# A hybrid decoder layer: gate products on half the array's rows, and two chunks' weight sums on another engine

## The chip, the cores and the metric

The kernel runs on one core of a Trainium2 chip. The core has five engines that work beside each other: TensorE (PE; its weight loads are listed apart as PEld), VectorE (DVE), ScalarE (ACT), GpSimd (POOL) and SyncE (SP), which here only issues DMAs. ScalarE and GpSimd issue a few DMAs too. The metric is the device time of one execution in microseconds (us); a profile of one further execution shows what each engine did and when.

## The reference

One layer over 1040 tokens (16 learned meta tokens and 1024 inputs) of width 1024, in float32:

```python
u = rmsnorm(h, g_pre_mix)
z = u @ w_in                                  # q | k | v | x_rec | y_rec
attn = sliding_window_attention_with_sinks(q, k, v, sinks)   # 8 heads, window 128
xr = causal_depthwise_conv(x_rec, conv_w, conv_b)            # 512 channels
gate_r = einsum("btnc,ncd->btnd", xb, w_a) + b_a             # 8 blocks of 64 channels
gate_i = einsum("btnc,ncd->btnd", xb, w_x) + b_x
r, i = sigmoid(gate_r), sigmoid(gate_i)
log_a = -8 * r * softplus(-lam);  a = exp(log_a)
hr = scan(a, sqrt(1 - a * a) * (i * xr))                     # h_t = a_t h_(t-1) + u_t
mix = concat([attn, gelu(y_rec) * hr]) @ w_out
h = h + rmsnorm(mix, g_post_mix)
f = square(relu(rmsnorm(h, g_pre_ffn) @ w_ff1)) @ w_ff2      # 1024 -> 4096 -> 1024
out = (h + rmsnorm(f, g_post_ffn))[16:]
```

Each of the two gates multiplies 8 separate blocks of 64 channels by a matrix of 64x64 of its own.

## The kernel before, in words

**Products in three parts.** Every float32 operand is split into a high part (a ScalarE copy to fp32r, line 96) and a low part (VectorE, source minus high part, line 99), and `mm3` (lines 123 to 129) multiplies high by high, high by low, low by high into one PSUM bank. So each product in the profile stands three times, at L125, L126 and L127, and each operand costs one ScalarE and one VectorE pass.

**Order.** A scheduler orders each engine's instructions by data dependence and a priority. The helper `behind` (line 106) adds an order without a wait across engines; `lut` (line 81) chains the ScalarE table functions in program order. Buffers are slots of a tag with a fixed number (line 55: two for "raw", four for "ws" and "d", two for "e", eight for "c", and so on); a load into a slot waits until the last reader of the old content is done, and SP's queue is worked in order.

**First stage, up to about 200 us.** Norm, transposes and the input projection; then attention over four head pairs. `scores` makes the scores, the softmax and the divisions on ScalarE and VectorE; `attend` transposes the probabilities on TensorE, splits them (L96, L99), masks both parts with GpSimd selects (L609) and multiplies by V (L620). Between them TensorE works on "fills" (`next_fill`, line 694): projections of the q, x and y columns (`project`), whose results are copied out of PSUM (y: L676 in `fill_y`). The small parameters (conv_w, conv_b, b_a, b_x, lambda) are loaded as eight rows (lines 355 to 358), transposed (L469) and kept as columns `prm`: column 5 is b_a, column 6 is b_x.

**Gates (lines 717 to 749), about 201 to 221 us.** The 512 channels are four groups of 128 on the partitions, two blocks of 64 each. For each gate and group the two 64x64 matrices stand on the diagonal of a 128x128 matrix that is zero elsewhere (`graw`; a GpSimd memset, four DMAs), and this is split into `gh` and `gl`. `gates(c)` splits the group's input `xc[c]`, multiplies in three pieces of 348, 348 and 344 columns for each of the two gates (18 products a group, 72 in all), applies a Sigmoid to each piece out of PSUM, and multiplies the second gate by the input (L749).

**Recurrence and output projection, about 221 to 330 us.** In pairs of groups: `decay` (Exp, Tanh on ScalarE), `recur` (a Sqrt, L762, L763 and the scan L764 on VectorE), Gelu of y, `rec_out` (L769 and a split into the operand `at`). Between these, the rows of w_out are loaded and split (`split_wo`). Then `out_mm`, `out_norm` (L853 to L867) and the transposes of the next operand (`u2_tiles`, L879).

**Feed-forward, from about 330 us.** It is computed by a scheme with seven products for 2x2 blocks of the matrices, which needs sums of blocks. `prep_a(p)` (line 928) prepares chunk p of 16 of the first weight matrix: two loads of 512 KB (`r0` in a "raw" slot, `r1`), the sums a22 + a21 and a11 - a21 (L905, via `combine`), the split of r0, a11 - a22 from the summed values, its split into an "e" slot, a12 minus that, and a store of r1 to `s_dram` that GpSimd issues (L950). The sums of activations t2 and t3, and their splits into `ot2` and `ot3`, are made by `t_sums` (line 1047), whose last quarter stands between `prep_a(0)` and `prep_a(1)`; TensorE multiplies ot2 with each chunk's "e" operand and ot3 with its "ws" operand (lines 1084 to 1094), with a copy of the bank in between (L1090). `t_rest` (line 1070) makes four further sums behind the chunks and stores two of them, as four DMAs from SP, to `t4_dram` (L1081). Then follow the second weight matrix and the final norm.

Of the kernel before, what the change touches and what calls it, by code (L numbers as in the profile page):

```python
# [37 lines left out]
def hybrid_layer(  # L38
# [19 lines left out]
    def slot(tag, shape, dt=F32):  # L58
        uid[0] += 1
        return slab.tile(shape, dt, tag=tag, name=f"{tag}{uid[0]}", bufs=bufs[tag])  # L60
# [4 lines left out]
    def bank(tag, shape=(P, 512)):  # L65
        uid[0] += 1
        return ps.tile(list(shape), F32, tag=tag, name=f"ps_{tag}{uid[0]}")

    def f32(ap):
        return ap.bitcast(F32)  # L70
# [23 lines left out]
    def split(hi, lo, src, eng=None):  # L94
        if eng is None:
            nc.scalar.copy(hi, src)  # L96
        else:
            eng.tensor_copy(hi, src)
        low = nc.vector.tensor_tensor(lo, src, f32(hi), op=ALU.subtract).ins  # L99
        mark[0] = low.name  # L100
        return low
# [4 lines left out]
    def behind(name, *inss):  # L106
        for ins in inss:
            tc.add_manual_dep(
                ins, name,
                mybir.DependencyInfo(  # L110
                    mybir.DependencyClass.NoSync, mybir.DependencyReason.DATA
                ),
                reason="order",
            )
# [239 lines left out]
    nc.sync.dma_start(nsink, attn_sinks[0].partition_broadcast(P))  # L354
    prm_r = slot("d", [8, 512])
    nc.sync.dma_start(prm_r[0:4, :], conv_w[0])
    for i, src in enumerate((conv_b, b_a, b_x, lru_lambda)):
        nc.sync.dma_start(prm_r[4 + i : 5 + i, :], src)


    vk = [slot("b", [P, 8, P], F32R) for _ in range(2)]
# [172 lines left out]
    def at_pair(cp):  # L534
        for half in range(2):
            at[half][cp] = pair("b", [P, 2, 512])


    def scores(j, half, q):

        sn = slot("c", [P, 2, 4, P + 1])
        negm = small.tile([P, 2, 4], F32, name="negm", tag="negm")
        den = small.tile([P, 2, 4], F32, name="den", tag="den")
        rden = small.tile([P, 2, 4], F32, name="rden", tag="rden")
        for h in range(2):
            nc.gpsimd.tensor_copy(
                sn[:, h, :, P], nsink[:, j + 4 * h : j + 4 * h + 1].to_broadcast([P, 4])
            )
        for h in range(2):
            for bp in range(2):  # L550
                sp_ = bank("s", (P, 2, 256))

                def qk(dst, b, hi, lo):
                    c = slice(b * P, (b + 1) * P)
                    nc.tensor.matmul(
                        dst, q[h][:, c], hi, start=True, stop=False,
                        skip_group_check=True,
                    )
                    nc.tensor.matmul(
                        dst, q[h][:, c], lo, start=False, stop=True,  # L560
                        skip_group_check=True,
                    )

                for i in range(2):
                    b = 4 * half + 2 * bp + i
                    if b == 0:
                        qk(sp_[:, i, 0:P], b, km[:, h, :], km[:, 2 + h, :])
                        qk(sp_[:, i, P:256], b, khh[h][:, 0:P], kl[h][:, 0:P])
                    else:
                        c = slice((b - 1) * P, (b + 1) * P)  # L570
                        qk(sp_[:, i, :], b, khh[h][:, c], kl[h][:, c])
                s_ = sn[:, h, 2 * bp : 2 * bp + 2, 0:P]
                nc.scalar.copy(s_, sp_[:, :, P:256])
                nc.vector.copy_predicated(
                    s_, above_i.rearrange("p (a b) -> p a b", a=1).to_broadcast([P, 2, P]),
                    sp_[:, :, 0:P],
                )
                if half == 0 and bp == 0:
                    w = slice(0, P - NMETA)
                    nc.vector.copy_predicated(sn[:, h, 0, w], above_i[:, w], far)  # L580
            nc.vector.tensor_reduce(
                negm[:, h, :], sn[:, h], axis=mybir.AxisListType.X, op=ALU.min
            )
            for k in range(4):
                lut(
                    sn[:, h, k, :], sn[:, h, k, :], AF.Exp, scale=-1.0,
                    bias=negm[:, h, k : k + 1], accum_out=den[:, h, k : k + 1],
                )
            nc.vector.reciprocal(rden[:, h, :], den[:, h, :])
            nc.vector.tensor_tensor(  # L590
                sn[:, h, :, 0:P], sn[:, h, :, 0:P],
                rden[:, h, :].to_broadcast([P, 4, P]), op=ALU.mult,
            )
        return sn
# [57 lines left out]
            )  # L652
        xc[c] = y

    ys = [None] * NLRU

    def fill_q(j):
        def run(w):
# [11 lines left out]

    def fill_y(c):
        def run(w):
            y = slot("b" if c == 1 else "d", [P, T])

            def sink(acc, t0, n):
                nc.vector.tensor_copy(y[:, t0 - NMETA : t0 - NMETA + n], acc)  # L676

            project(w, REAL2, sink)
            ys[c] = y
        return run  # L680
# [22 lines left out]
    for j in range(NPAIR):  # L703
        for half in range(2):
            if j % 2 == 0 and half == 0:
                at_pair(j // 2)
            sn = scores(j, half, qs[j])
            if True:
                with deferred(FILL_LAG):
                    next_fill()  # L710
            if prev is not None:
                attend(*prev)
            prev = (j, half, sn)
    attend(*prev)


    graw = slot("e", [P, 2, NLRU, P])
    behind(last_pow[0], nc.gpsimd.memset(graw, 0.0).ins)
    for i, w in enumerate((w_a, w_x)):
        for s in range(2):  # L720
            r = slice(HD * s, HD * s + HD)
            nc.sync.dma_start(
                graw[r, i, :, r], w[0, s::2].rearrange("n c d -> c n d")
            )
    gh = slot("e", [P, 2, NLRU, P], F32R)
    gl = slot("b", [P, 2, NLRU, P], F32R)
    split(gh, gl, graw)

    rg = [None] * NLRU

    def gates(c):
        ch, cl = pair("b", [P, TT])
        split(ch, cl, xc[c])
        rg[c] = []
        for i in range(2):
            t_ = slot("c", [P, TT])
            for t0, n in ((0, 348), (348, 348), (696, 344)):
                flip[0] += 1
                acc = bank(("s", "pt", "o")[flip[0] % 3])
                mm3(  # L740
                    acc[:, :n], (gh[:, i, c, :], gl[:, i, c, :]),
                    (ch[:, t0 : t0 + n], cl[:, t0 : t0 + n]), True, True,
                )
                lut(
                    t_[:, t0 : t0 + n], acc[:, :n], AF.Sigmoid,
                    bias=prm[:, c, 5 + i : 6 + i],
                )
            rg[c].append(t_)
        nc.vector.tensor_tensor(t_, t_, xc[c], op=ALU.mult)  # L749

    av = [None] * NLRU

# [37 lines left out]

    for c in range(NLRU):
        gates(c)
    for _ in range(2):
        next_fill()
    for cs in ((0, 1), (2, 3)):
        for c in cs:
            decay(c)
# [127 lines left out]
    s_dram = dpool.tile([16, P, 4, 256], F32, name="s_dram")  # L925


    def prep_a(p, late=None):
        r0 = slot("raw", [P, 4, 256])
        w1_load(r0, 0, p, 0, 2)  # L930
        r1 = slot("a" if 2 <= p < 6 else "d", [P, 4, 256])
        w1_load(r1, 1, p, 0, 2)
        a11, a21, a12, a22 = r0[:, :, LO], r0[:, :, HI], r1[:, :, LO], r1[:, :, HI]
        sums = [
            combine(a22, a21, a22, ALU.add), combine(a21, a11, a21, ALU.subtract)
        ]
        if late:
            behind(late, *sums)
        hi, lo = pair("ws", [P, 4, 256])
        if p in a11_early:  # L940
            split(hi[:, :, HI], lo[:, :, HI], a21)
            first = a11_early[p]
        else:
            split(hi, lo, r0)
            first = hi[:, :, LO], lo[:, :, LO]
        combine(a11, a22, a11, ALU.subtract)
        hl = slot("e", [P, 2, 4, P], F32R)
        split(hl[:, 0], hl[:, 1], a11)
        combine(a12, a12, a11, ALU.subtract)
        nc.gpsimd.dma_start(s_dram[p], r1)  # L950
        return first, (hl[:, 0], hl[:, 1]), (hi[:, :, HI], lo[:, :, HI])
# [118 lines left out]
    def t_rest(k):  # L1070
        i = k % 2
        if k < 2:
            behind(mark[0], combine(u2f[1][i], u2f[1][i], u2f[0][i], ALU.subtract))
        elif k < 4:
            behind(mark[0], combine(t2[i], u2f[0][2 + i], t2[i], ALU.subtract))
        else:
            hl = pair("a", [P, 2, 512])
            late = mark[0]
            behind(late, split(*hl, t2[i]))
            for n in range(2):  # L1080
                nc.sync.dma_start(t4_dram[:, n, 2 * i : 2 * i + 2, :], f32(hl[n]))  # L1081

    raw_b, raw_c = {}, {}
    for p in range(16):
# [319 lines left out]
```

## Time and profile before

| | us |
|---|---|
| time, median of 3 runs | 965.29 (964.68 to 965.95) |
| the profiled execution | 966.98 |
| its span in the profile | 965.3 |
| busy in it: PE / PEld / DVE / ACT / POOL | 947.6 / 795.0 / 651.6 / 503.2 / 120.5 |
| 201 to 221 us (20 us): PE / DVE / ACT / POOL | 20.0 / 7.5 / 14.7 / 0.0 |
| 221 to 270 us (49 us): PE / DVE / ACT / POOL | 48.8 / 40.7 / 36.0 / 0.0 |
| 350 to 377 us (27 us): PE / DVE / ACT / POOL | 25.6 / 19.7 / 12.2 / 1.6 |

TensorE's granted clock is 1.00 in all these stretches. Matmuls are pipelined: a 512-column product is listed with 0.39 us, but the next one starts 0.23 us after it. So how long TensorE needs is read from the distance between starts, and a wait is a larger distance. An idle time in square brackets after a timeline row is that of the engine before the row, and the name behind the arrow is what ended it.

### The profile page before, as it was taken

What the parts mean: (1) busy time and instruction counts of PE and PEld (TensorE: products, weight loads), DVE (VectorE), ACT (ScalarE), POOL (GpSimd) and SP (SyncE); (2) the same over time, 40 slices, a digit from 0 to 9 for tenths busy, and PEclk for the clock granted to TensorE, in tenths of its full rate; (3) what the DMA queues carried; (4) which work ended last, traced back from release to release, by engine and by line L of the source; (5) the groups of instructions that cost most, each with busy time, mean ns of one, the idle gap of its engine ahead of it and who ended that gap; (6) DMA issues with size and microseconds to landing.
All of it is one profiled execution on the core that took longest, in us unless ns stands there. A gap on an engine that the chain in (4) does not pass through costs nothing.

```text
span 965.3 us, 12356 instructions
## 1 busy us (share of the span) xinstructions
PE 947.6 (98%) x4718; PEld 795.0 (82%) x4718; DVE 651.6 (68%) x833; ACT 503.2 (52%) x845; POOL 120.5 (12%) x183
## 2 busy tenths in 40 slices
PE   6999999999999999999999999999999999999996
PEld 6999999888878877888888888888888888888885
DVE  5567988856865695665654455468557676779884
ACT  6546765567744663443555566654433343436441
POOL 4202544500011100000000000000111100001201
PEclk9999999999999999999999999999999999999999
DMA  8121010013235457576423264324687765547934
GB/s 278 37 56 40 24 44 23 25 49 81 88 129 156 157 173 237 180 254 201 173 87 106 92 202 130 103 91 122 163 186 183 193 210 206 184 144 195 240 66 88
DMA packets 88155, 130.14 MB, mean 135 GB/s; under 512 B 13688, under 2 KB 52616, under 8 KB 88096
## 3 DMA queue, kind: packets, MB, share of 16 engines
q1 hardware_dynamic: 79504, 106.54, 34.0%
q0 software_dynamic: 8160, 21.51, 10.8%
q10 hardware_dynamic: 432, 1.31, 0.4%
q8 instruction: 37, 0.61, 0.3%
q14 instruction: 22, 0.18, 0.1%
HBM read 109.93 MB, written 18.87 MB: 133 GB/s over the span
## 4 chain that ended last, share of the span: by engine, by line
PE 81%; DVE 8%; ACT 4%; issue 3%; DMA 3%; POOL 1%; SPq 0%; DVEq 0%; ACTq 0%; POOLq 0%
PE ps_acc L125 9%; PE ps_acc L127 9%; PE ps_acc L126 9%; PE ps_pt L125 6%; PE ps_pt L127 5%; PE ps_pt L126 5%; PE ps_s L127 5%; PE ps_s L125 5%; PE ps_s L126 5%; PE ps_o L125 5%; PE ps_o L126 5%; PE ps_o L127 5%; ACT c L82 1%; PE ps_acc L253 1%; PE ps_o L620 1%
## 5 line engine op out<-in xcount | busy, mean ns | idle before, releaser
L96 ACT CAST ws<-raw 128x1024 fp32r<-128x1024 f32 (+1 forms) x68 | 69.6, 1024 | 120.7 <-PE ps_o L126 50.5
L99 DVE TENSOR_TENSOR ws<-raw,ws 128x1024 fp32r<-128x1024 f32 (+1 forms) x69 | 82.3, 1193 | 46.0 <-ACT ws L96 45.9
L125 PE MATMUL ps_acc<-a,ws 128*128 128x256 f32 (+2 forms) x256 | 85.8, 335 | 0.1
L126 PE MATMUL ps_acc<-a,ws 128*128 128x256 f32 (+2 forms) x256 | 85.4, 334 | 0.0
L127 PE MATMUL ps_acc<-a,ws 128*128 128x256 f32 (+2 forms) x256 | 84.9, 332 | 0.0
L99 DVE TENSOR_TENSOR b<-b,b 128x1024 fp32r<-128x1024 f32 (+2 forms) x48 | 57.5, 1199 | 32.3 <-PE ps_o L126 19.4
L96 ACT CAST ws<-e 128x1024 fp32r<-128x1024 f32 x41 | 42.9, 1045 | 65.4 <-PE ps_o L126 45.9
L96 ACT CAST b<-b 128x1024 fp32r<-128x1024 f32 (+2 forms) x47 | 48.8, 1037 | 37.3 <-DVE b L905 37.3
L99 DVE TENSOR_TENSOR ws<-e,ws 128x1024 fp32r<-128x1024 f32 x41 | 50.1, 1222 | 19.6 <-ACT ws L96 19.6
L609 POOL TENSOR_SCALAR_AFFINE_SELECT c<-c 128x512 fp32r<-128x512 f32 x64 | 52.6, 837 | 71.8 <-ACT c L96 61.9
L125 PEld LDWEIGHTS ps_acc<-a,ws 128*128 128x128 f32 x256 | 48.2, 188 | 4.6 <-ACT c L396 0.4
L127 PEld LDWEIGHTS ps_acc<-a,ws 128*128 128x128 f32 x256 | 48.2, 188 | 4.3
L126 PEld LDWEIGHTS ps_acc<-a,ws 128*128 128x128 f32 x256 | 48.2, 188 | 4.0
L125 PE MATMUL ps_acc<-ws,b 128*128 128x512 f32 (+1 forms) x120 | 46.2, 386 | 0.0
L127 PE MATMUL ps_acc<-ws,b 128*128 128x512 f32 (+1 forms) x120 | 46.2, 385 | 0.0
L126 PE MATMUL ps_acc<-ws,b 128*128 128x512 f32 (+1 forms) x120 | 46.1, 384 | 0.0
L125 PE MATMUL ps_pt<-ws,b 128*128 128x512 f32 x112 | 44.3, 395 | 0.0
L126 PE MATMUL ps_pt<-ws,b 128*128 128x512 f32 x112 | 44.1, 394 | 0.0
L127 PE MATMUL ps_pt<-ws,b 128*128 128x512 f32 x112 | 44.0, 393 | 0.0
L125 PE MATMUL ps_s<-ws,b 128*128 128x512 f32 x110 | 43.5, 395 | 0.0
L127 PE MATMUL ps_s<-ws,b 128*128 128x512 f32 x110 | 43.4, 394 | 0.0
L126 PE MATMUL ps_s<-ws,b 128*128 128x512 f32 x110 | 43.3, 394 | 0.0
(394 smaller groups left out, 2658.9 us busy)
## 6 DMA issues: line engine op xcount, KB each, us to landing
raw<-in_w_ff_dram SPq DMA_DIRECT2D x61, 512.0 KB, 3.8
e<-in_w_ff_dram SPq DMA_DIRECT2D x45, 512.0 KB, 3.8
d<-in_w_ff_dram SPq DMA_DIRECT2D x12, 512.0 KB, 3.8
s_dram<-d POOLq DMA_DIRECT2D x12, 512.0 KB, 4.0
raw<-in_w_in_dram SPq DMA_DIRECT2D x9, 512.0 KB, 4.6
c<-in_x_dram SPq DMA_DIRECT2D x8, 512.0 KB, 9.1
d<-in_x_dram SPq DMA_DIRECT2D x8, 512.0 KB, 4.8
out_dram<-raw SPq DMA_DIRECT2D x8, 512.0 KB, 2.6
```

The lines of the kernel that those rows point to most:

```text
L82: ins = nc.scalar.activation(*args, **kwargs).ins
L96: nc.scalar.copy(hi, src)
L99: low = nc.vector.tensor_tensor(lo, src, f32(hi), op=ALU.subtract).ins
L125: nc.tensor.matmul(dst, lh, rh, start=start, stop=False, skip_group_check=True)
L126: nc.tensor.matmul(dst, lh, rl, start=False, stop=False, skip_group_check=True)
L127: last_mm[0] = nc.tensor.matmul(dst, ll, rh, start=False, stop=stop, skip_group_check=True).ins.name
L253: last_mm[0] = nc.tensor.matmul(acc[:, :n], w[k // 2][:, kc, :], u[kc][k % 2][:, t0 : t0 + n], start=k == 0 and kc == 0, stop=k == last an ...
L609: nc.gpsimd.affine_select(out=p_[:, :, s], in_=f32(p_[:, :, 0]), pattern=[[0, 4], [g, P]], compare_op=op, fill=0.0, base=0, channel_multip ...
L620: nc.tensor.matmul(po[:, oc : oc + n], v, p_[:, pc : pc + n], start=first and k == 0, stop=last and k == 1, skip_group_check=True,)
```

## The change

The diff has five parts.

1. **Gate matrices and products.** `graw` has no zeros any more: it holds, for each group, 64 rows for the first block and 64 for the second, and in its columns the two gates side by side, for the second block in the other order. `gates(c)` multiplies each half of the partitions by itself: product s = 0 takes rows 0 to 63 and writes gate r of block 0 and gate i of block 0 to the 128 partitions of one bank; s = 1 takes rows 64 to 127 and writes gate i of block 1 and gate r of block 1 to another bank. The number of products, their columns and the Sigmoids stay the same. The split of the weights is half as large, and its ScalarE part is put behind the softmax of the last pair (`gate_after`); the memset is gone.
2. **Copies.** Since each bank now mixes the gates, `gather(c)` copies 64x1040 three times a group: two by VectorE into a new tile `gi`, one by GpSimd. Then comes the product with the input as before. The gathers of groups 0 and 1 stand between the gates; those of groups 2 and 3 are put behind the first copy of the third y projection (`y_copies`).
3. **Biases.** b_a and b_x are loaded in two DMAs each, half by half, into the matching rows.
4. **Weight sums.** For p = 1 and 2 the two sums at the head of `prep_a` go to GpSimd. For other p they are put behind the low part of the split of the last chunk that had a whole one (`a_low`).
5. **t4.** The four stores to `t4_dram` are issued by GpSimd instead of SP. The y projection of the third group gets a "b" slot instead of a "d" slot.

```diff
-    for i, src in enumerate((conv_b, b_a, b_x, lru_lambda)):
-        nc.sync.dma_start(prm_r[4 + i : 5 + i, :], src)
+    for i, src in ((4, conv_b), (7, lru_lambda)):
+        nc.sync.dma_start(prm_r[i : i + 1, :], src)
+    for i, src in enumerate((b_a, b_x)):
+        for s in range(2):
+            nc.sync.dma_start(
+                prm_r[5 + s : 6 + s, :].rearrange("o (c t k) -> t o c k", t=2, k=HD)[i ^ s],
+                src.rearrange("o (c t k) -> t o c k", t=2, k=HD)[s],
+            )
...
-            y = slot("b" if c == 1 else "d", [P, T])
+            y = slot("b" if c in (1, 2) else "d", [P, T])
...
+            gate_after = last_lut[0]
             sn = scores(j, half, qs[j])
...
-    graw = slot("e", [P, 2, NLRU, P])
-    behind(last_pow[0], nc.gpsimd.memset(graw, 0.0).ins)
+    graw = slot("e", [P, NLRU, P])
     for i, w in enumerate((w_a, w_x)):
         for s in range(2):
-            r = slice(HD * s, HD * s + HD)
             nc.sync.dma_start(
-                graw[r, i, :, r], w[0, s::2].rearrange("n c d -> c n d")
-            )
-    gh = slot("e", [P, 2, NLRU, P], F32R)
-    gl = slot("b", [P, 2, NLRU, P], F32R)
-    split(gh, gl, graw)
+                graw[HALF[s], :, HALF[i ^ s]],
+                w[0, s::2].rearrange("n c d -> c n d"),
+            )
+    gw = slot("e", [P, 2, NLRU, P], F32R)
+    behind(gate_after, nc.scalar.copy(gw[:, 0], graw).ins)
+    nc.vector.tensor_tensor(gw[:, 1], graw, f32(gw[:, 0]), op=ALU.subtract)
...
-        for i in range(2):
-            t_ = slot("c", [P, TT])
-            for t0, n in ((0, 348), (348, 348), (696, 344)):
+        z = [slot("c", [P, TT]) for _ in range(2)]
+        for t0, n in ((0, 348), (348, 348), (696, 344)):
+            acc = []
+            for s in range(2):
                 flip[0] += 1
-                acc = bank(("s", "pt", "o")[flip[0] % 3])
-                mm3(
-                    acc[:, :n], (gh[:, i, c, :], gl[:, i, c, :]),
-                    (ch[:, t0 : t0 + n], cl[:, t0 : t0 + n]), True, True,
+                acc.append(bank(("s", "pt", "o")[flip[0] % 3]))
+            for k, (a, b) in enumerate(((0, ch), (0, cl), (1, ch))):
+                for s in range(2):
+                    nc.tensor.matmul(
+                        acc[s][:, :n], gw[HALF[s], a, c, :], b[HALF[s], t0 : t0 + n],
+                        start=k == 0, stop=k == 2, skip_group_check=True,
+                    )
+            for s in range(2):
+                lut(
+                    z[s][:, t0 : t0 + n], acc[s][:, :n], AF.Sigmoid,
+                    bias=prm[:, c, 5 + s : 6 + s],
                 )
...
-        nc.vector.tensor_tensor(t_, t_, xc[c], op=ALU.mult)
+        rg[c] = z
+    def gather(c):
+        z, gi = rg[c], slot("b" if c > 1 else "c", [P, TT])
+        first = nc.vector.tensor_copy(gi[HALF[0]], z[0][HALF[1]]).ins
+        nc.gpsimd.tensor_copy(z[0][HALF[1]], z[1][HALF[1]])
+        nc.vector.tensor_copy(gi[HALF[1]], z[1][HALF[0]])
+        nc.vector.tensor_tensor(gi, gi, xc[c], op=ALU.mult)
+        rg[c] = z[0], gi
+        return first
...
         gates(c)
-    for _ in range(2):
-        next_fill()
+        if c < 2:
+            gather(c)
+    next_fill()
+    for c in (2, 3):
+        behind(y_copies[2], gather(c))
+    next_fill()
...
-        sums = [
-            combine(a22, a21, a22, ALU.add), combine(a21, a11, a21, ALU.subtract)
-        ]
-        if late:
-            behind(late, *sums)
+        if p in (1, 2):
+            nc.gpsimd.tensor_tensor(a22, a21, a22, op=ALU.add)
+            nc.gpsimd.tensor_tensor(a21, a11, a21, op=ALU.subtract)
+        else:
+            sums = [
+                combine(a22, a21, a22, ALU.add), combine(a21, a11, a21, ALU.subtract)
+            ]
+            if late or a_low[0]:
+                behind(late or a_low[0], *sums)
...
-            split(hi, lo, r0)
+            a_low[0] = split(hi, lo, r0).name
...
-                nc.sync.dma_start(t4_dram[:, n, 2 * i : 2 * i + 2, :], f32(hl[n]))
+                nc.gpsimd.dma_start(t4_dram[:, n, 2 * i : 2 * i + 2, :], f32(hl[n]))
```

Code elsewhere is the same. In the order as built, TensorE's 64-row products stand in four blocks of 18, one for each group, with 128-row fills before and after each.

More of the change, by code (lines that the diff above doesn't have):

```diff
@@ L653, in conv @@
         xc[c] = y
-    ys = [None] * NLRU
+    ys, y_copies = [None] * NLRU, {}
     def fill_q(j):
@@ L672, in run @@
         def run(w):
-            y = slot("b" if c == 1 else "d", [P, T])
+            y = slot("b" if c in (1, 2) else "d", [P, T])
             def sink(acc, t0, n):
-                nc.vector.tensor_copy(y[:, t0 - NMETA : t0 - NMETA + n], acc)
+                ins = nc.vector.tensor_copy(y[:, t0 - NMETA : t0 - NMETA + n], acc).ins
+                y_copies.setdefault(c, ins.name)
             project(w, REAL2, sink)
@@ L733, in gates @@
         split(ch, cl, xc[c])
-        rg[c] = []
-        for i in range(2):
-            t_ = slot("c", [P, TT])
-            for t0, n in ((0, 348), (348, 348), (696, 344)):
+        z = [slot("c", [P, TT]) for _ in range(2)]
+        for t0, n in ((0, 348), (348, 348), (696, 344)):
+            acc = []
+            for s in range(2):
                 flip[0] += 1
-                acc = bank(("s", "pt", "o")[flip[0] % 3])
-                mm3(
-                    acc[:, :n], (gh[:, i, c, :], gl[:, i, c, :]),
-                    (ch[:, t0 : t0 + n], cl[:, t0 : t0 + n]), True, True,
-                )
-                lut(
-                    t_[:, t0 : t0 + n], acc[:, :n], AF.Sigmoid,
-                    bias=prm[:, c, 5 + i : 6 + i],
-                )
-            rg[c].append(t_)
-        nc.vector.tensor_tensor(t_, t_, xc[c], op=ALU.mult)
+                acc.append(bank(("s", "pt", "o")[flip[0] % 3]))
[9 more added lines that the diff above has]
+                    bias=prm[:, c, 5 + s : 6 + s],
+                )
+        rg[c] = z
[7 more added lines that the diff above has]
+        return first
     av = [None] * NLRU
@@ L925, in hybrid_layer @@
     s_dram = dpool.tile([16, P, 4, 256], F32, name="s_dram")
+    a_low = [None]
     def prep_a(p, late=None):
```

## The prediction, as put on record before the result

> **What bounds the kernel now.** I read the page first (busy times, then the chain that ended last), then TensorE's waits, then the timelines of the three stretches that the change touches: the gates (201 to 270 us), the end of attention (150 to 190) and the first weight chunks (336 to 377).
>
> ```profile
> PE 947.6 (98%) x4718; PEld 795.0 (82%) x4718; DVE 651.6 (68%) x833; ACT 503.2 (52%) x845; POOL 120.5 (12%) x183
> ...
> PE 81%; DVE 8%; ACT 4%; issue 3%; DMA 3%; POOL 1%; SPq 0%; DVEq 0%; ACTq 0%; POOLq 0%
> ```
>
> TensorE is busy 98% of the span and makes 81% of the chain. A kernel like this gets shorter in two ways only: fewer TensorE slots, or fewer of its waits. The waits:
>
> ```profile
> PE ps_s L127 <- DVE e L99: 0.7, 1, 0.7
> PE ps_acc L125 <- ACT a L1090: 0.7, 1, 0.7
> PE ps_o L620 <- POOL c L609: 0.6, 1, 0.6
> PE ps_pt L125 <- ACT b L96: 0.2, 1, 0.2
> ```
>
> Those are all after the first 40 us. Short gaps are not listed there, so I also took start-to-start times from the timeline: a 512-column product normally follows the last after 0.23 us. What exceeds that is 0.8 us at 188.1, 0.7 us at 268.8 to 270.4, and 2.5 us between 350 and 377; from 377 to the end almost nothing.
>
> **The gate products (72 of them).** In the timeline of the gates:
>
> ```profile
> 208.14 0.32 PE L125 MATMUL ps_s<-b,e 128*128 128x348 f32 x1
> 208.30 0.32 PE L126 MATMUL ps_s<-b,e 128*128 128x348 f32 x1
> 208.46 0.32 PE L127 MATMUL ps_s<-b,b 128*128 128x348 f32 x1
> 208.62 0.32 PE L125 MATMUL ps_pt<-b,e 128*128 128x348 f32 x1
> ```
>
> One starts every 0.16 us (0.158), so 72 take 11.4 us. After the change there are again 72, each on 64 rows: the upper or the lower half of the array. Their number doesn't fall; a gain comes only where a product of one half runs beside one of the other. The built order decides how often. Written as halves 0 and 1: channel group 0 alternates throughout (17 changes of half); group 1 runs 000111 and then alternates (13); groups 2 and 3 run 000 111 000 111 00 11 0 1 (7 each). That is 44 changes, 24 followers on the same half, and 4 first ones. Bounds: if a product of the other half starts at once and only followers on the same half wait, I count 9, 11, 12 and 12 slots, 44 x 0.158 = 7.0 us, a gain of 4.4. If nothing overlaps, the gain is 0. Between them stands how closely weight loads follow each other, since each product still has its own:
>
> ```profile
> 96.11 0.28 PE L555 MATMUL ps_s<-km,b 128*128 128x128 f32 x1
> 96.22 0.27 PE L559 MATMUL ps_s<-km,b 128*128 128x128 f32 x1
> 96.33 0.28 PE L555 MATMUL ps_s<-b,b 128*128 128x128 f32 x1
> ```
>
> 128-column products, which stream much less, still start 0.11 us apart. If this is the load and the halves share it, 24 x 0.158 + 48 x 0.11 = 9.1 us, a gain of 2.3. I take the middle of 2.3 and 4.4: 3.4 us.
>
> Against it stand 8 passages between 128-row and 64-row work (the products come in four blocks between fills). The nearest row is the only work on few rows:
>
> ```profile
> 55.08 0.38 PE L306 MATMUL ps_o<-ident,d 128*128 128x128 f32 x2
> 55.29 0.38 PE L306 MATMUL ps_s<-ident,d 128*128 128x128 f32 x2
> 55.60 0.41 PE L469 MATMUL ps_o<-ident,d 8*128 8x8 f32 x4
> ```
>
> Two transposes take 0.21 us up to the next pair, and 0.31 before the 8-row ones: 0.10 us for the passage. Eight are 0 to 0.8 us; I take 0.3. The products gain **3.1 us**. [...]
>
> **From the gates to the output projection.** The chain of waits from 218.7 to 269.4 is ScalarE and VectorE work (Sigmoid, table loads, Exp, scan, splits), so a faster TensorE could simply wait at 269. But ScalarE's 24 Sigmoids at 0.45 us fill only 10.7 of the 16.3 us from 204.85 to 221.15; 3.7 us are waits for products (0.32, 1.38, 1.95), 1.1 a cast that now stands ahead. The last Sigmoid should end about 3 us sooner. In the new VectorE order the w_out splits (1.2 us each) stand ahead of the second recurrence pair instead of inside it, so the chain after that is no longer. The added copies: eight VectorE ones of 64x1040, between 0.69 us (128x1024 cast, L98) and 1.13 (128x1040, L644) each, 5.5 to 9 us, fall into VectorE's idle time between 201 and 229, which sums to 17 us (6.82, 1.56, 0.67, 3.61, 1.41, 3.23):
>
> ```profile
> 208.14 1.24 DVE L99 TENSOR_TENSOR b<-b,b 128x1040 fp32r<-128x1040 f32 x1 [6.82 <-ACT b L96]
> ```
>
> The four GpSimd copies stand on an engine that does nothing from 189 to 274. Groups 0 and 1 are copied while groups 2 and 3 are in their Sigmoids. I cost both at nothing; without that cover the last group's DVE copy, GpSimd copy and product would be 3 to 4 us on the chain. Of the 0.7 us wait at 269 I let **0.5 us** go (0.7 at best; minus 3.1 if the chain stays put).
>
> **End of attention.** Splitting the gate weights halves in size (128x1024 to 128x512: ScalarE 1.1 to 0.6, VectorE 1.2 to 0.7), but moves from slack (ScalarE at 51, VectorE at 196.7) into the softmax of the last pair, which ends in GpSimd's selects and TensorE's 0.8 us at 188. With it comes the ScalarE issue of the g_post_mix load (0.38). Replaying the new VectorE order over its row times, the transposes' splits there move forward by as much, and the last split before the selects ends within 0.6 us of today. I take 0, and 0.6 either way. The memset leaves (0.95 us of idle GpSimd). The two extra small loads on SP delay its next weight loads by about 2.6 us (1.3 us apart today) at 21 us; those weights are used after 55. Nothing.
>
> **The weight sums.** The 2.5 us between 350 and 377 are mainly two waits:
>
> ```profile
> 357.45 0.50 PE L125 MATMUL ps_acc<-b,ws 128*128 128x512 f32 x1 [0.67 <-ACT a L1090]
> ...
> 373.38 0.50 PE L127 MATMUL ps_s<-b,e 128*128 128x512 f32 x1 [0.73 <-DVE e L99]
> ```
>
> The first is the copy of a bank out before the next product may add to it; the new order puts two products (0.46 us) there, so about 0.4 stays. The second comes from chunk 3: its load waits for chunk 1's buffer, which VectorE frees only at 361.5 in a run of work without a gap. Four VectorE sums of 0.69 us (2.8 us) go to GpSimd, and chunk 1 is worked off first. The price: VectorE reaches chunk 1's next step at 351.2 and then waits for GpSimd, and behind that step stand the last quarter of t2's split (VectorE and ScalarE both), which TensorE needs at 354.06. Chunk 1's second load is issued at 344.9 and lands about 4.8 us later (raw loads here: 4.5 median), at 349.7. Two sums of X each end at 349.7 + 2X, the split 2.1 us later. GpSimd shows no sum of 512; the nearest are the selects:
>
> ```profile
> 166.85 1.92 POOL L609 TENSOR_SCALAR_AFFINE_SELECT c<-c 128x512 fp32r<-128x512 f32 x3 [0.24 <-DVE c L99]
> 184.93 4.20 POOL L609 TENSOR_SCALAR_AFFINE_SELECT c<-c 128x512 fp32r<-128x512 f32 x3 [2.67 <-DVE c L99]
> ```
>
> 0.64 us each with VectorE quiet, 1.4 beside it. A sum reads two inputs: 0.64 to 2.8 us; I take 1.3. Then the split is done at 354.4 and TensorE waits 0.3 to 0.7 us; chunk 1's buffer comes free about 359.5, chunk 3 is ready before its turn at 372, and of 2.5 us some 1.4 stay: **1.1 us** gained (2.0 at X = 0.64, 1.2 lost at 2.8). [...] The other sums' ties follow the order that VectorE already shows from 377 on, where it idles 3 us a chunk. The four t4 stores go from SP to GpSimd's queue, where they cost about 0.53 us each as the s_dram stores do and can hold back the s_dram stores behind them; those are 8 us apart and are read 100 us later. Nothing, at worst 1 us.
>
> **Sum.** 3.1 + 0.5 + 1.1 = 4.7 us. The profiled execution took 966.98 us (span 965.3) and would take 962.3; against the median of 965.29 it is **960.6 us**.
>
> **Rivals.**
> - Full overlap: a product of the other half starts at once. 4.4 - 0.3 + 0.7 + 1.3 = 6.1 us, 959.2. For it: halves share neither rows nor banks. Against: the 0.11 us. [...] 25%.
> - No overlap: products stay at 11.4 us, passages cost 0.3; only 0.5 + 1.1 come: 964.0. 10%.
> - The gain is lost at 269: copies or splits hold the recurrence where it was, TensorE waits 3.1 us more; 1.1 us remains with the passages paid: 964.2. 10%.
> - GpSimd's sums take 2.8 us: 3.1 + 0.5 - 1.2 = 2.4 us, 962.9. 8%.
> - Slower: each change of half costs what the passage at 55.3 did. 52 x 0.10 = 5.2 us more on the products, less 0.7 and 1.0 elsewhere: 968.8. It decides from about 0.07 us a change. Only that one row speaks for it, and there the number of rows changed. 10%.
> - The forecast: 37%.
>
> **Numbers.** A measurement here tells about 0.2% (1.9 us) from no change. Faster: the forecast, full overlap and most of the slow sums, 0.70; within 0.2%: no overlap and the lost gain, 0.18; slower 0.12. The range runs from full overlap with the best sums to the cases with little gain: 958.4 to 965.2; it leaves out the slower rival.
>
> **What would show it.** Gate products of alternating halves starting under 0.1 us apart on average (right), at 0.16 (no overlap) or above (slower). TensorE's wait at 269 gone, the one before L125 near 354 under 1 us and none at 372; GpSimd's sums at 1.3 us. A wait of 3 us before the first kc 6 product of the output projection, or sums over 2 us, would make me wrong.

## The result and the profile after

The changed kernel takes 963.58 us (median of 12 runs, 961.73 to 966.76) beside 965.58 us of the kernel before on the same chip (12 runs, 964.68 to 966.87): a ratio of 0.998, 95% interval 0.9971 to 0.9989. It is faster by 2.0 us (1.1 to 2.8), where the forecast was 4.7. In a second comparison it was 963.13 to 965.64 us, ratio 0.9971 (0.9956 to 0.9986). The time lies inside the range and on the forecast side, but under half of the forecast gain came.

The page of the profiled execution (963.36 us, span 961.4) looks like the one before, a little shorter on TensorE and longer on VectorE and GpSimd; first the busy times, then the chain:

```profile
PE 942.7 (98%) x4718; PEld 788.9 (82%) x4718; DVE 658.4 (68%) x837; ACT 502.4 (52%) x845; POOL 134.2 (14%) x194
...
PE 90%; DVE 3%; ACT 3%; POOL 1%; DMA 1%; issue 1%; DVEq 0%; SPq 0%; POOLq 0%; ACTq 0%
```

The two profiled executions also differ in their first 25 us, by 1.1 us at the starts of TensorE's products. That seems to be chance: the kernel that changes only the weight sums has the code of before in that stretch and is 1.0 us ahead there too, and the profiled execution of before was 1.7 us above its median. So I compare stretches, by the distance between the starts of TensorE's products, and not the spans.

**Gates.** The timeline of the same place as in the prediction:

```profile
200.26 0.43 PE L753 MATMUL ps_s<-b,e 64*128 64x348 f32 x1
200.27 0.42 PE L753 MATMUL ps_pt<-b,e 64*128 64x348 f32 x1
200.53 0.32 PE L753 MATMUL ps_s<-b,e 64*128 64x348 f32 x1
200.53 0.31 PE L753 MATMUL ps_o<-b,e 64*128 64x348 f32 x1
200.69 0.32 PE L753 MATMUL ps_pt<-b,e 64*128 64x344 f32 x1
```

Two products start together, within 15 ns. The next two follow after 0.26 us, and from there on each pair 0.16 us after the last: 72 products in 36 slots. The passages are dearer than the slots suggest: around each block of 18 the first start, the second, the first 128-row start behind it and the next are each about 0.1 us late, 0.4 us a block. Together the four blocks take 36 x 0.158 + 4 x 0.4 = 7.3 us instead of 11.4.

**Output projection.** The wait at 269 us is gone; TensorE's waits between 195 and 400 us are these two (line, what ended it, us in total, times, longest):

```profile
PE ps_acc L126 <- DVE b L99: 2.2, 1, 2.2
PE ps_acc L125 <- ACT a L1123: 0.2, 1, 0.2
```

**Weight sums.** The first of them is new, and it is t2's last quarter. GpSimd's timeline there, then VectorE's:

```profile
343.17 2.32 POOL L964 TENSOR_TENSOR d<-raw,d 128x512 f32<-128x512 f32 x1 [4.84 <-DMA raw<-in_w_ff_dram]
345.57 1.30 POOL L965 TENSOR_TENSOR raw<-raw 128x512 f32<-128x512 f32 x1
346.82 1.30 POOL L964 TENSOR_TENSOR a<-raw,a 128x512 f32<-128x512 f32 x1
```

```profile
346.90 1.78 DVE L932 TENSOR_TENSOR raw<-d,raw 128x512 f32<-128x512 f32 x1 [2.57 <-POOL raw L965]
348.60 1.75 DVE L99 TENSOR_TENSOR ws<-raw,ws 128x512 fp32r<-128x512 f32 x1
350.28 0.75 DVE L99 TENSOR_TENSOR b<-a,b 128x256 fp32r<-128x256 f32 x2
```

VectorE waits 2.57 us for chunk 1's sums, as the prediction had it. But its next two steps take 1.7 us each, start to start, while chunk 2's sums run on GpSimd (that these are the cause is tested below); only then comes the split that TensorE waits for. The same two steps in the kernel before:

```profile
357.92 0.68 DVE L905 TENSOR_TENSOR raw<-d,raw 128x512 f32<-128x512 f32 x1
359.13 0.68 DVE L99 TENSOR_TENSOR ws<-raw,ws 128x512 fp32r<-128x512 f32 x1
```

And TensorE does not come back at full speed. Its timeline:

```profile
350.75 0.73 PE L126 MATMUL ps_acc<-b,e 128*128 128x512 f32 x1 [2.23 <-DVE b L99]
351.27 0.63 PE L127 MATMUL ps_acc<-b,e 128*128 128x512 f32 x1
351.70 0.63 PE L125 MATMUL ps_acc<-b,e 128*128 128x512 f32 x1
```

The products now start 0.43 us apart, not 0.23. The table by stretches shows why (span, busy time of PE, PEld, DVE, ACT, POOL with counts, granted clock, DMA share, GB/s):

```profile
350.70:354.30 3.60, 3.55 (x9) 2.78 (x10) 3.60 (x5) 0.00 (x0) 0.59 (x1) 0.53 0.00 0
```

The granted clock is 0.53 here: in the record it is at half for 3.41 us from 350.85 on, and at 1.0 everywhere else between 13 and 958 us. The page's row of forty digits hides it, since one slice is 24 us long. In the kernel before the clock never fell in the body of the run.

So from 325 to 375 us TensorE loses 4.5 us to waits and slow products (2.4 for the wait, 1.7 for the products at the low clock, 0.5 around a bank copy), where in the kernel before the waits of chunks 1 and 3 cost 2.5. The gates and the wait at 269 gave about 4.3 us, and 2.0 went back here.

### The profile page after: what moved, and what is told of

Read it like the earlier page. It is cut to its first block, busy times and chain, and to the rows that moved or that the text cites. A ratio compares the mean times of both kernels' runs of the same rounds, so it can differ in the third digit from the quotient of the medians.

```text
span 961.4 us, 12393 instructions
## 1 busy us (share of the span) xinstructions
PE 942.7 (98%) x4718; PEld 788.9 (82%) x4718; DVE 658.4 (68%) x837; ACT 502.4 (52%) x845; POOL 134.2 (14%) x194
## 4 chain that ended last, share of the span: by engine, by line
PE 90%; DVE 3%; ACT 3%; POOL 1%; DMA 1%; issue 1%; DVEq 0%; SPq 0%; POOLq 0%; ACTq 0%
PE ps_acc L126 10%; PE ps_acc L125 10%; PE ps_acc L127 10%; PE ps_s L127 6%; PE ps_s L126 6%; PE ps_s L125 6%; PE ps_pt L125 6%; PE ps_pt L126 6%; PE ps_pt L127 6%; PE ps_o L127 5%; PE ps_o L125 5%; PE ps_o L126 5%; ACT c L82 1%; PE ps_o L627 1%; PE ps_acc L253 1%
```

## The experiments

Theory A, before the runs: the gates' half gives all it promised, and the sums on GpSimd lose about 2 us through VectorE's order, GpSimd's interference and the clock. Rival B: the gates gave only 2 us and the sums cost nothing.

**The two halves apart.** The sums of p = 1, 2 given back to VectorE:

```diff
-        if p in (1, 2):
+        if p in ():
```

> The changed kernel with the weight sums of the second and third chunk pair given back to VectorE, behind the last quarter of t2 as before; the gates, the copies, the ties and the store queue stay changed. Theory A (the gates gain about 4.1 us and the wait at 269 us 0.7 us, and the sums on GpSimd lose 2 to 2.8 us of it, since VectorE waits in order for GpSimd with t2's last quarter queued behind, and TensorE's clock then falls for 3.4 us): 960.8 us, about 2.8 us under the changed kernel's 963.6, and TensorE's wait at 348 to 351 us and the low clock are gone. Rival B (the gates gave only about 2 us in the median, and the sums cost nothing that counts): 963.6 us.

Only the sums, ties and t4 stores, put into the kernel before:

```diff
+        if p in (1, 2):
+            nc.gpsimd.tensor_tensor(a22, a21, a22, op=ALU.add)
+            nc.gpsimd.tensor_tensor(a21, a11, a21, op=ALU.subtract)
...
-                nc.sync.dma_start(t4_dram[:, n, 2 * i : 2 * i + 2, :], f32(hl[n]))
+                nc.gpsimd.dma_start(t4_dram[:, n, 2 * i : 2 * i + 2, :], f32(hl[n]))
```

> The kernel before with only the second half of the change: weight sums of the second and third chunk pair on GpSimd, the ties, and t4's stores in GpSimd's queue; gates as before. Theory A: 2 to 2.8 us over before, 967.6 to 968.4 us, with a TensorE wait of 2 us or more on t2's last quarter some 5 us later than in the changed kernel, and a stretch of half clock behind it. Rival B: 965.6 us, no change.

Only the gates: the changed kernel with sums, ties and stores as before:

```diff
-        if p in (1, 2):
+        if p in ():
...
-            if late or a_low[0]:
-                behind(late or a_low[0], *sums)
+            if late:
+                behind(late, *sums)
...
-                nc.gpsimd.dma_start(t4_dram[:, n, 2 * i : 2 * i + 2, :], f32(hl[n]))
+                nc.sync.dma_start(t4_dram[:, n, 2 * i : 2 * i + 2, :], f32(hl[n]))
```

> The kernel before with only the first half of the change: 64-row gate products, copies by VectorE and GpSimd, their order; sums, ties and stores as before. Theory A: 4.8 us under before, 960.8 us, the same as with the sums alone given back. Rival B: about 963.6 us. A third theory (the stores in GpSimd's queue or the ties matter): this kernel differs by over 0.5 us from the one with only the sums given back.

Measured, beside 965.45 of before: sums back 961.81 us (ratio 0.9966, 0.9954 to 0.9979), sums only 968.47 (1.0029, 1.0019 to 1.0039), gates only 961.52 (0.9963, 0.9949 to 0.9976). Rival B falls, but theory A had too much for the gates: it forecast 960.8 us for the kernels with sums back and gates only, which came out 1.0 and 0.7 us slower. The gates' half gains 3.6 us (2.3 to 4.9); the sums' half alone loses 2.8 us (1.8 to 3.8), and this although the clock stayed at 1.0 in its profiled execution, where theory A expected it to fall. Sums back and gates only differ by 0.3 us, inside both intervals, and VectorE's, ScalarE's and TensorE's order is the same in the two: the ties and t4's queue cost and gain nothing that shows.

**The order behind the sums.** GpSimd keeps the sums, but the steps that read them first, the split of one and the first difference, stand behind t2's last quarter:

```diff
-            split(hi[:, :, HI], lo[:, :, HI], a21)
+            high = nc.scalar.copy(hi[:, :, HI], a21).ins
+            low = nc.vector.tensor_tensor(
+                lo[:, :, HI], a21, f32(hi[:, :, HI]), op=ALU.subtract
+            ).ins
+            mark[0] = low.name
+            if late:
+                behind(late, high, low)
...
-        combine(a11, a22, a11, ALU.subtract)
+        ins = combine(a11, a22, a11, ALU.subtract)
+        if late:
+            behind(late, ins)
```

> The changed kernel with the sums left on GpSimd, but VectorE's and ScalarE's steps that read them (split of the sum, first difference) put in order behind the last quarter of t2, so that it no longer queues behind a wait for GpSimd. Theory A: the wait of 2.2 us on t2's last quarter and the low clock go; 960 to 961.5 us, 2 us or more under the changed kernel. Rival C (GpSimd's sums are late for TensorE in any order, or VectorE beside them is too slow): the wait only moves to the sums' products, 963 us or more. Rival B: 963.6 us.

962.26 us (ratio 0.9971, 0.996 to 0.9983): a miss of my range, between theory A and rival C. The wait on t2's last quarter and the low clock are gone, but two others came, and VectorE shows why (L1060 is the addition that reads a PSUM bank):

```profile
344.46 2.65 DVE L99 TENSOR_TENSOR b<-a,b 128x256 fp32r<-128x256 f32 x2 [0.23 <-ACT b L96]
347.04 0.68 DVE L1060 TENSOR_TENSOR b<-ps_pt,b 128x512 f32<-128x512 f32 x1
347.64 1.72 DVE L99 TENSOR_TENSOR b<-a,b 128x1024 fp32r<-128x1024 f32 x1
```

These do not wait for GpSimd's results, and yet beside its sums the two quarter splits take 2.65 us instead of 0.75, and the large split 1.72 instead of 1.22. The step in the middle, one of whose inputs is in PSUM, keeps its 0.68. TensorE waits 0.9 us on the "e" operand of chunk 1, which is late now, and 1.6 on that of chunk 3, which stands on VectorE behind a sum that waits for its load.

**Interference by itself.** To the gates-only kernel, GpSimd work that feeds nobody; the order on the other engines does not move. First nine additions, in a buffer of their own:

```diff
+    spare = slot("spare", [P, 224])
+    for n in range(9):
+        nc.gpsimd.tensor_tensor(spare, u2f[1][2][:, n % 2, 288:], u2f[0][0][:, n % 2, 288:], op=ALU.add)
```

> The kernel with only the gates' half of the change (961.5 us), and nine useless additions of 128x224 on GpSimd, both inputs from SBUF, from about 342 us on: they feed nobody, so nobody waits for them, and the order on every other engine is the same. Theory A (GpSimd's reads and VectorE's additions of two SBUF inputs exclude each other, so that VectorE is slowed by GpSimd's sums also without any wait for a result): VectorE's steps at 342 to 349 us take up to three times as long, its work ends 2 to 4 us later, and the time is 962 to 964 us. Rival C (only the wait for results in VectorE's order counts): VectorE's steps keep 0.69, 0.76 and 1.22 us, 961.5 us.

Then memsets in their place, behind one addition of a single column that holds them at the same point:

```diff
+    spare = slot("spare", [P, 224])
+    nc.gpsimd.tensor_tensor(
+        spare[:, 0:1], u2f[1][2][:, 1, 511:512], u2f[0][0][:, 0, 0:1], op=ALU.add
+    )
+    for n in range(18):
+        nc.gpsimd.memset(spare, 1.0)
```

> As the kernel with nine useless additions on GpSimd, with eighteen useless memsets of 128x224 in their place, some 5 us of GpSimd's work at the same place that reads nothing from SBUF. Theory A with reads as the cause: VectorE's steps keep their durations of 0.69, 0.76 and 1.22 us, 961.5 us. Rival (any work of GpSimd slows VectorE): the steps are longer as beside the additions, 962 to 964 us.

964.45 us with the additions (ratio 0.9987, 0.9978 to 0.9996), 961.27 with the memsets (0.995, 0.9938 to 0.9963). On the same chip, additions that nobody needs cost 3.2 us more than memsets that nobody needs, and those cost nothing against gates only. (The clock fell in the profiled execution with the additions too, to a mean of 0.53 from 358 to 361.6 us, so not all of the 3.2 is VectorE's delay.) VectorE beside the additions, then beside the memsets:

```profile
343.20 1.69 DVE L932 TENSOR_TENSOR a<-c,c 128x256 f32<-128x256 f32 x2
344.82 1.42 DVE L99 TENSOR_TENSOR b<-a,b 128x768 fp32r<-128x768 f32 x1
```

```profile
341.93 0.75 DVE L932 TENSOR_TENSOR a<-c,c 128x256 f32<-128x256 f32 x2
342.60 0.95 DVE L99 TENSOR_TENSOR b<-a,b 128x768 fp32r<-128x768 f32 x1
```

The same two steps: 1.69 and 1.42 us instead of 0.75 and 0.95. So it is not GpSimd's being busy. What additions do and memsets don't is read SBUF, and compute on what they read; no run parts these two, and how either holds VectorE up is not shown.

**The clock.** Useless products in TensorE's wait, so that it is not idle:

```diff
+    spare = bank("o")
+    for kc in range(3):
+        mm3(
+            spare, (a12_early[3][0][:, kc, :], a12_early[3][1][:, kc, :]),
+            (b21[kc // 2][0][:, kc % 2, :], b21[kc // 2][1][:, kc % 2, :]),
+            kc == 0, kc == 2,
+        )
```

> The changed kernel with nine extra products (three quarters of p=3's second product again, into a bank that nobody reads) put into TensorE's queue just ahead of the products that wait for t2's last quarter: 9 x 0.232 = 2.1 us of useless work inside a wait of 2.4 us. Theory A (the wait itself lets the clock fall to half for 3.4 us, which costs 9 x 0.195 = 1.75 us in the executions in which it falls): the low clock is gone from the trace and the time falls, 961.9 to 962.7 us against 963.6. Rival (the clock record has no consequence, or falls for another reason): useless work cannot help, 963.6 to 964.0 us.

964.49 us (ratio 0.9988, 0.9978 to 0.9999), above what either theory had: no gain. The clock stays at 1.0 in the trace, but the scheduler also reordered VectorE and ScalarE behind the products, and TensorE waits 1.3 us at 353.4 and 1.1 at 365.4 instead. The run proves nothing about the clock's price. So I tied the order (eight `behind` ties, mainly on the copies, splits and products of the first chunks) and ran it with and without the nine products:

> The same nine useless products in TensorE's wait (the changed kernel, its sums on GpSimd), now with the order of the steps behind them on TensorE, VectorE and ScalarE tied to that of the changed kernel but for swaps of neighbours, so that nothing else moves with them. If the low clock costs what its products' spacing says (1.75 us in the executions in which it falls, perhaps half of them): 0.9 to 1.75 us under the kernel with the same ties and no extra products, about 962 us. Rival: what comes next (the split of the second pair's operand on VectorE, done at 355 us) is late anyway and takes the gain: no more than 0.4 us under it.

> The same ties without the extra products: the changed kernel's order by hand. Both theories: 963.6 us within 0.5, the wait of about 2.4 us on t2's last quarter is there, and in some executions 3.4 us of half clock.

965.76 us with them (ratio 1.0, 0.9988 to 1.0012; 962.68 to 969.76), 962.42 without (0.9964, 0.9952 to 0.9976): filling the wait made it slower by 3.3 us, which neither theory had, and the ties alone came out 1.2 us faster than expected. In the trace with the products the stretch from 325 to 375 us loses only 0.8 us, but TensorE, which has 2.1 us of extra work behind it, then waits 0.7, 0.8 and 0.8 us for splits of later chunks between 403 and 431. Even with the ties, VectorE works ten of its steps and ScalarE four in another order there than with the ties alone. What that spread of 7 us comes from I can't say. By filling, the price of the low clock stays open.

The ties alone gave something better. TensorE, VectorE and ScalarE work in the same order there as in the changed kernel, so its six executions are in effect further ones of that kernel, and their 962.42 us lies in its spread. In the profiled execution the wait on t2's last quarter is there, 2.0 us by the starts instead of 2.4, and the clock does not fall. To see how often it falls in the changed kernel, that one ran once more:

> The changed kernel itself once more, for a second profiled execution: whether its clock falls depends, by theory A, on how the wait of 2.4 us lies in the windows of 3.41 us in which the clock record moves. If the clock stays up, the stretch from 325 to 375 us, by the starts of TensorE's products, loses about 2.5 us to waits in place of 4.5, with the same wait of 2.2 to 2.4 us on t2's last quarter; if it falls again, 4.5 us. The time: 963.6 us within 1 us, with a spread of 3 us or more, as before. Rival (the clock falls in every execution and the waits alone spread): the same 4.5 us and a low clock at the same place.

963.13 us (960.74 to 965.68), and in the profiled execution the clock fell again, for 3.41 us from 351.62 on, after a wait of 2.25 us by the starts; the stretch lost 4.5 us again. The same 50 us in the changed kernel and in the one with the ties alone:

```profile
325.00:375.00 50.00, 47.55 (x206) 38.07 (x205) 37.67 (x55) 24.76 (x43) 10.59 (x11) 0.97 0.59 192
```

```profile
325.00:375.00 50.00, 47.97 (x215) 38.59 (x214) 38.47 (x56) 25.54 (x45) 10.17 (x12) 1.00 0.61 199
```

206 products in one, 215 in the other: 9 x 0.23 = 2.1 us. 0.4 of it is the shorter wait, and the 1.7 that remain are what the products' spacing says of the low clock (seven starts 0.195 us late and the first 0.29). With VectorE's sums (the kernel with the sums given back) it is 213. So in this execution, without the low clock, the GpSimd sums are no worse there than VectorE's; with it they lose 1.6 us. That does not hold for every kernel: in the one with only the sums the clock stayed at 1.0 as well, and TensorE still waited from 325 to 380 us

```profile
PE ps_acc L126 <- DVE b L99: 2.3, 1, 2.3
PE ps_acc L125 <- ACT b L96: 0.8, 1, 0.8
```

which with a bank copy behind them makes 4.1 us by the starts, against 2.5 in the kernel before.

How often the clock falls without a profile can be estimated from the mean granted clock that the record has for each execution: one low period takes 0.0018 off it. The mean is 0.9964 over the 12 executions of the changed kernel in the first comparison and 0.9974 over the 7 in the second, beside 0.998 for the kernel before. So a low period came in most executions of the first and in about a third of those of the second. It is a rough estimate: the profiled executions also end at half clock, for 3.0 us in the changed kernel's and 3.5 in that of the kernel before. The kernel with memsets, in whose trace the clock stays up until 954 us, has 0.997 in all five executions.

**One half of the array.** All gate products on rows 0 to 63:

```diff
-                        acc[s][:, :n], gw[HALF[s], a, c, :], b[HALF[s], t0 : t0 + n],
+                        acc[s][:, :n], gw[HALF[0], a, c, :], b[HALF[0], t0 : t0 + n],
```

> The kernel with only the gates' half of the change (961.5 us), but all 72 gate products read rows 0 to 63 of their operands, so that every product sits in the same half of the array; the gates of the upper heads are thus computed from the lower heads' rows. Nothing else moves. Theory A (the gain comes from products in different halves running at the same time): the products take turns, 72 x 0.158 = 11.4 us in place of 36 x 0.158 = 5.7, and with unchanged passages the time is 966 to 967 us, slower than before. Rival (64-row products are shorter by themselves, or the gain lies elsewhere): 961.5 us.

966.58 us (ratio 1.0011, 1.0002 to 1.0019), some 5 us over gates only:

```profile
200.50 0.32 PE L753 MATMUL ps_pt<-b,e 64*128 64x348 f32 x1
200.66 0.32 PE L753 MATMUL ps_o<-b,e 64*128 64x348 f32 x1
```

One at a time, 0.16 us apart, and the passages stay. The gates' gain is the overlap of the two halves, and without it their half of the change would have been slower than before.

**A better version.** Gates only, all sums on VectorE, but the second chunk pair is worked off ahead of ot3's splits and of the third pair, and TensorE takes p = 1's first product ahead of p = 0's second:

```diff
-    for i in range(2):
-        behind(urgent, split(*ot3[i], t3[i]))
     wa[1] = prep_a(1, urgent)
+    for i in range(2):
+        behind(e_low[1], split(*ot3[i], t3[i]))
...
-            wa[p + 2] = prep_a(p + 2, None if p else urgent)
+            wa[p + 2] = prep_a(p + 2, None if p else e_low[1])
...
-        product(ya[p], wa[p][1], ot2, False)
-        nc.scalar.copy(block("12", p), ya[p])
+        for k in ((0, 1), (), *((k,) for k in range(2, 16)))[p]:
+            product(ya[k], wa[k][1], ot2, False)
+            nc.scalar.copy(block("12", k), ya[k])
```

Here `e_low[p]` is the low part of chunk p's "e" split.

> The kernel with only the gates' half of the change (961.5 us), and VectorE's order for the first chunks changed: the sums, differences and splits of the second chunk pair go ahead of the splits of ot3 and ahead of the third pair's, all on VectorE; TensorE takes the second pair's first product ahead of the first pair's second. Theory A (the waits of 0.84, 0.48 and 0.90 us at 350 to 367 us come from VectorE's order, not from its load): 959.3 us. Rival (VectorE is full there, the waits move to the products with ot3 or to the third pair): 961 to 962 us.

959.25 us (ratio 0.993, 0.9918 to 0.9943): 6.6 us under before, 4 to 5 under the changed kernel. TensorE's waits from 340 to 380 us with the sums given back, and in this one:

```profile
PE ps_s L127 <- DVE e L99: 0.7, 1, 0.7
PE ps_acc L125 <- ACT a L1123: 0.7, 1, 0.7
PE ps_s L125 <- ACT e L96: 0.3, 1, 0.3
```

```profile
PE ps_s L125 <- ACT a L1124: 0.2, 1, 0.2
```

It has 223 products in the 50 us. So the waits that the change wanted to remove by taking work off VectorE go with all sums left on it. They were a matter of order; the edit moves steps on VectorE and a product on TensorE, and no run tells which of the two it needs.

## Why the prediction was wrong, and where it was right

- **The gates** ("3.1 us"): 4.1 by the trace, and two errors that partly cancel. Overlap gave 5.7 us (72 products in 36 slots), more than the bound of 4.4, because the 24 "followers on the same half" do not wait either. The passages, taken at 0.3 us of at most 0.8, cost 1.6: each block has two late starts going in and two coming out, and the one row I used shows one. That the sum still came near 3.1 is in part luck. The trace has 0 to 15 ns between the two halves of a pair, and 0.4 us for each block there and back.
- **The wait at 269** ("0.5 us"): it went, 0.7 us; small gaps of 0.5 us in all came at 230 and 237. The last Sigmoid ends at 216.97 instead of 221.15; 1.1 us of that is the first 25 us, and the other 3.1 are the "about 3 us" that I expected, so the chain did move. The copies cost nothing, as said: 0.70 us each on VectorE, 1.48 to 1.52 on GpSimd. With gates only, the half measures 3.6 us (2.3 to 4.9) against 3.1 + 0.5.
- **End of attention** ("0, and 0.6 either way"): 0.80 us of wait before, 0.75 after.
- **Ties and t4** ("nothing"): 0.3 us between two kernels that differ only in these, inside the intervals. The small loads, also put at nothing, were not tested apart.
- **The weight sums** ("1.1 us gained"): this step failed. In the first comparison it lost 1.4 to 1.8 us against the sums given back (by ratios and by medians), in the second 0.5 to 1.3; the intervals overlap, so the size stays rough. By itself it lost 2.8 (1.8 to 3.8). The chain that I drew (VectorE waits for GpSimd, t2's last quarter stands behind) was right; its terms were not. (1) I had "the split 2.1 us later" than the sums; it is 4.2, since VectorE's two steps before it take 1.7 us each beside chunk 2's sums instead of 0.6. A price for work beside GpSimd was in my own row (selects of 0.64 us alone and 1.4 beside VectorE), but I let it count for GpSimd alone. (2) The two sums took 2.32 and 1.30 us, 1.0 more than 2 x 1.3, since the first ran beside VectorE's additions. Against both, the load landed 0.9 us sooner than I reckoned. So TensorE waited 2.4 us, not "0.3 to 0.7". (3) A longer wait was priced at its length only. It also let the clock fall in both profiled executions of the changed kernel, 1.7 us more. Chunk 3's wait went as forecast; the 2.5 us that stood there became 4.5 instead of 1.4.
- **The rivals**: "full overlap" was the right reading of the gates, "GpSimd's sums take 2.8 us" came nearest for the other half. I let each stand alone; both came true, and their sum with the clock is the result. The 1.3 us of gain that "full overlap" has for the weight sums is shown by no run: they lost 0.5 to 1.8. "Slower" and "no overlap" had nothing for them: pairs start 0.158 us apart, on average 0.08 us a product. Of the signs that I had named, the wait before t2's last quarter ("under 1 us") and the sums ("at 1.3 us") failed, at 2.4 and at up to 2.32 us.

Shown by runs: the size of each half, the overlap as the gates' cause, and that additions on GpSimd make VectorE's steps beside them longer (1.69 us instead of 0.75 for the same two) and memsets don't. By comparing executions only: the low clock's 1.7 us. Open: how often exactly the clock falls in executions without a profile (the spread of 5 us in the changed kernel fits it and does not prove it), and why the sums alone lose 2.8 us in the kernel before but 0.5 to 1.8 here.

## What to carry to other kernels

Before moving VectorE work to GpSimd, count which VectorE steps with two SBUF inputs will run beside it, and price those as they ran here beside additions (128x512: 1.7 us instead of 0.68); then ask whether VectorE was short of time there or only badly ordered. The products on half the rows paid here only by their partners on the other half (two in 0.16 us; on one half alone, one in 0.16 us), and each block of them cost 0.4 us, so blocks should be few and long. A wait of over 2 us on a busy TensorE cost 1.7 us beyond its length in both profiled executions of the changed kernel; with only the sums the clock stayed at 1.0 after a wait of 2.3 us.

## What the hardware showed beside that

- **The clock fell after a wait of 2.2 to 2.4 us.** The low period within the changed kernel's run lasts 3.413 us, and the times between other changes of the record are multiples of it (337.92 us = 99 x 3.413 and 604.16 = 177 x 3.413; in the kernel before, 945.49 = 277 x 3.413). Cut into stretches of that length by the record's own edges, TensorE's products (0.232 us each) covered 30% and 31% of the stretch before the fall in the two executions of the changed kernel, and 39% in the kernel with useless additions; with 42% (ties alone), 45% and 48% (sums only, two stretches in a row) the clock stayed. In the two executions of the changed kernel, one such stretch held all of the wait.
- **TensorE's gate products started in another order than the built one.** The first six products of group 1 stand in the built order as three of one half, then three of the other, and in the trace they start in pairs all the same (205.55 and 205.56, 205.81 and 205.82, 205.97 and 205.98).
- **GpSimd's two-input addition** of 128x512 took 1.30 us in the changed kernel where VectorE waited or started its own step later, and up to 2.32 where it met VectorE's additions.
